# Adding the taps of a depthwise convolution by accumulating transfers, in three tiles instead of two

## The chip, the core and the metric

The kernel runs on one core of a Trainium2 chip. It uses five queues of instructions: TensorE (PE in the profile, with its weight loads as PEld), VectorE (DVE), ScalarE (ACT), GpSimd (POOL) and SyncE (SP), which issues the transfers. The metric is the device time of one execution in microseconds (us), lower is better.

## The reference

One layer of a hybrid decoder, for 1024 positions of 1024 channels in fp32: a modulated RMS norm, one wide input product, a convolution group and a recurrent group beside each other, and an output product.

```
h = rmsnorm(x, norm_g) * (1 + scale) + shift
cv, cg, cs, lx, ls = split(h @ w_in)              # five times 1024 channels

v = cv * sigmoid(cg)
v = causal_depthwise_conv(v, dw_w, dw_b)          # 31 taps a channel
v = silu(layernorm(v, cln_g, cln_b))              # over the channels
y_conv = (v @ pw2_w + pw2_b) * silu(cs)

xs = causal_depthwise_conv(lx, sc_w, sc_b)        # 4 taps
r, i = sigmoid(xs @ wr + br), sigmoid(xs @ wi + bi)   # 8 blocks of 128 channels
a = exp(-8 * r * softplus(-lam))
hs = scan(a, sqrt(1 - a * a) * i * xs)            # h_t = a_t h_{t-1} + b_t
y_lru = hs * silu(ls)

x = x + (1 + gate) * (concat(y_conv, y_lru) @ w_out)
return rmsnorm(x, final_g)
```

The change concerns the convolution of 31 taps and, in a small way, where sums stand in PSUM.

## The kernel before

Channels lie on the 128 partitions and positions along the free dimension, so every activation is eight tiles of 128 x 1024 floats. Each fp32 product is made of three products of halves: a weight tile is split by ScalarE into a rounded upper part `whi` (a cast), and by GpSimd into the rest, `wlo` = raw - `whi`; the activation has `uh` and `ul` likewise. A weight tile is then 48 matmuls of 512 columns (8 blocks of channels, three products, two halves of the positions). Raw tiles, upper and lower parts have two buffers each.

The program isn't written in the order in which it runs. Each step is recorded as an `Op` with an engine, an assumed cost, a priority and the buffers that it reads and writes, and `Plan.order` lists the steps engine by engine: whenever an engine is free it takes the ready step with the lowest priority number for which there are buffers. The order of each queue is fixed by these assumed costs; at run time each engine goes through its queue in that order and waits where an operand isn't there. A pool of 47 buffers of one tile each (`big`) holds nearly all activations, and a buffer that the plan has freed is given to the next step that needs one.

The stages, in order: loading and modulation; the first products (`first`, by blocks of `FIRST`), with the sums of squares and their spread beside them; a long stretch over `slots` of the input product, in which each slot is one weight tile; the products of the recurrent group's gates (`gate`), scans and convolutions between them; the recurrent half of the output product (slots `lru`), beside which the layer norm runs; the second product of the convolution group (`pw2`, TensorE rows `papw` and `pbpw`); and the rest of the output product with the final norm.

The convolution of one tile is recorded by `conv_tile(i)`, as soon as its input `v` is there. There are two kinds:

- Tiles in `POOLED` (2 and 5): ScalarE multiplies the shifted input with each tap (tiles `cq`), and GpSimd adds the products one after another into the tile `c`.
- The other six: VectorE sums the taps by even and odd positions with a scheme of three half-length convolutions, in an accumulator `cacc` in PSUM of two banks, 15 + 15 + 14 taps of 512 positions, with copies by ScalarE and three additions behind it.

The finished tiles are added into `csum` in the order `SUMS`, by GpSimd and the last by VectorE. TensorE multiplies `csum` with a matrix of 1/1024 (`mean`); `layer_norm` subtracts it from the eight tiles, sums the squares, spreads the reciprocal root over the partitions (`lnbc`), and `quarters` splits the results for `pw2`.

GpSimd also does `wlo`, the products of the gate's modulation (`modw`, followed by a ScalarE step that sums them up) and most of `csum`. ScalarE also does `whi`, the evacuation of product tiles (`sig`, `scs`, `sls`, `xs`), and the gates' functions with loads of function tables. PSUM has a pool of three product tiles of two banks (`mm`) and one accumulator of two banks (`acc`), which the fourth of the first products, the token statistics, the convolution sums, `mean` and `lnbc` use in turn.

In the profile, L320 is the helper `TT` (additions, subtractions and products of two tensors, on either engine), L312 the helper `STT` (VectorE, a scalar times a tensor and an addition), L301 and L293 are ScalarE's `ACT`, and L438 is the matmul of a weight tile.

Of the kernel before, what the change touches and what calls it, by code (L numbers as in the profile page):

```python
# [9 lines left out]
F32 = mybir.dt.float32  # L10
# [35 lines left out]
POOLED = (2, 5)  # L46
# [6 lines left out]
SUMS = (0, 1, 3, 2, 4, 6, 5, 7)  # L53
QRES = 4
GM = 22
# [22 lines left out]
class Op:  # L78
    __slots__ = ("eng", "cost", "emit", "prio", "table", "bufs", "succ", "wait", "ready",
                 "seq", "reserve", "columns", "lock", "end", "psum")  # L80


class Plan:
# [23 lines left out]
    def op(self, eng, cost, emit, prio, r=(), w=(), table=None, after=(), reserve=0,  # L107
           columns=0, lock=False):
        o = Op()
        o.eng, o.cost, o.emit, o.prio, o.table = eng, cost, emit, prio, table  # L110
# [24 lines left out]
        o.psum = [(b, any(k[0] is b for k in w)) for b in o.bufs if b.pool in ("mm", "acc")]  # L135
        self.ops.append(o)
        return o

    def order(self):
# [19 lines left out]
        def done(o, end):  # L159
            o.end = until[o.eng] = end  # L160
# [14 lines left out]
        while left:  # L175
# [3 lines left out]
            for e in engines:  # L179
# [42 lines left out]
                if e == "POOL" and held["DVE"] > t + 1e-9:  # L222
                    waiting, until[e] = o, float("inf")
                    continue
# [24 lines left out]
def hymba_layer(ctx: ExitStack, tc: tile.TileContext, xT, c_row, vecs, mod_w, w_first, w_in,  # L249
# [11 lines left out]
    psacc = ctx.enter_context(tc.tile_pool(name="psacc", bufs=1, space=bass.MemoryType.PSUM))  # L261
# [8 lines left out]
    pools["acc"] = (psacc, "acc", [P, T], 1)  # L270
# [46 lines left out]
    def TT(prio, eng, out, a, b, op, n=T, r=(), w=(), reserve=0, after=()):  # L317
# [3 lines left out]
                    reserve=reserve, lock=not in_psum(r), after=after)  # L321

# [132 lines left out]
    def acc_tile(name, parts=2):  # L455
        return S.buf("acc", name, F32, parts)
# [187 lines left out]
    psf = [mm_tile(f"first{n}", 4) for n in range(3)] + [acc_tile("first3", 4)]  # L644
    psb = psf[3]
# [15 lines left out]
    def fw_mm(prio, ps, i, xh, xl, k, cols, after=()):  # L661
        _, wh, wl = fw[k - k % 2]

        def emit():
            for lhs, rhs, last in ((wh, xh, 0), (wh, xl, 0), (wl, xh, 1)):
                for a, b in cols:
                    pe.matmul(ps()[:, a:b], fw_part(lhs, k, i * P, i * P + P)(),  # L667
# [92 lines left out]
    st, wk = ctile("st", KT), halves(psb, H, T)  # L760

    def stats(sq, k):
        for b in range(KT):
            pe.matmul(psb()[:, H + b:H + b + 1], sq()[:, b * P:b * P + P], ones[:, 0:1],
                      start=k == 0 and b == 0, stop=k == len(sqs) - 1, skip_group_check=True)

    def spread_mm(a, e):
        for b in range(a // P, e // P):
            o = H + b * P - a
# [4 lines left out]
    ACT(RSP, lambda: st, lambda: psb()[:, H:H + KT], AF.Sqrt, KT, bias=eps_t, scale=1.0 / D,  # L774
        r=wk, w=[("st", 0)])
    S.op("DVE", 0.12, lambda: dve.reciprocal(st, st), RSP, [("st", 0)], [("st", 0)])
    for a, e in START:
        spread = S.op("PE", 0.22 * ((e - a) // P), lambda a=a, e=e: spread_mm(a, e), RSP,
                      [("st", 0)], wk, columns=4 * (e - a))
        ACT(RSP, part(rbc, a, e), part(psb, H, H + e - a), "copy", e - a, r=wk,  # L780
# [104 lines left out]

    def conv_tile(i):
# [19 lines left out]
        acc, b2 = acc_tile(f"cacc{i}"), bias2[:, i:i + 1]  # L906
        acc_e, acc_s, src_s = half(acc, 0), half(acc, 1), half(ci, 0)
# [8 lines left out]
        def every(o):  # L916
# [3 lines left out]
            w=[(acc, 0)])  # L920
        ACT(pr, acc_s, src_s, AF.Identity, H, scale=ws(0), bias=b2,
            r=[(ci, 0), ("V", 1), ("wsum", 0)], w=[(acc, 1)])
        for r in range(1, 16):
            STT(pr, cut(acc_e, r, H), cut(ev, 0, H - r), w(2 * r), cut(acc_e, r, H), ALU.mult,
                ALU.add, H - r, r=[vi, (acc, 0)], w=[(acc, 0)])
            STT(pr, cut(acc_s, r, H), cut(src_s, 0, H - r), ws(r), cut(acc_s, r, H), ALU.mult,
                ALU.add, H - r, r=[(ci, 0), (acc, 1)], w=[(acc, 1)])
        ACT(pr, every(1), acc_s, "copy", H, r=[(acc, 1)], w=[ci])
        ACT(pr, acc_s, od, AF.Copy, H, scale=w(1), r=[vi], w=[(acc, 1)])
        for r in range(1, 15):  # L930
            STT(pr, cut(acc_s, r, H), cut(od, 0, H - r), w(2 * r + 1), cut(acc_s, r, H), ALU.mult,
                ALU.add, H - r, r=[vi, (acc, 1)], w=[(acc, 1)])
        ACT(pr, every(0), acc_e, "copy", H, r=[(acc, 0)], w=[ci])
        TT(pr, "DVE", every(1), every(1), acc_e, ALU.subtract, H, r=[ci, (acc, 0)], w=[ci])
        TT(pr, "DVE", every(1), every(1), acc_s, ALU.subtract, H, r=[ci, (acc, 1)], w=[ci])
        TT(pr, "DVE", cut(every(0), 1, H), cut(every(0), 1, H), cut(acc_s, 0, H - 1), ALU.add,
           H - 1, r=[ci, (acc, 1)], w=[ci])
# [99 lines left out]
    def layer_norm():  # L1037
        pr = 45
        mean = acc_tile("mean")
# [14 lines left out]
        bc = acc_tile("lnbc")  # L1054
# [7 lines left out]
    for i, (s, ps) in enumerate(zip(FIRST, psf)):  # L1062
        j, p, bi = s[1] % KT, EVP + i, bias[:, i:i + 1]
        t = big_buf(f"first_u{i}", parts=4)
        for a, e in START:
# [4 lines left out]
            else:  # L1070
                for k in range(KT):
                    fw_mm(RSP + 60 + 0.1 * k, ps, i, uhs[k], uls[k], k, ((a, e),), after=[spread])
                TT(p, "DVE", part(t, a, e), part(ps, a, e), part(rbc, a, e), ALU.mult, n,
                   r=pk + halves(rbc, a, e), w=tk)
# [230 lines left out]
```

## Time and profile before

| | before |
|---|---|
| runs, us | 768.59, 771.37, 770.60 (median 770.60) |
| the profiled execution, us | 771.28 |
| its span, us | 769.4 |
| mean granted TensorE clock | 0.985 |
| busy: TensorE, VectorE, ScalarE, GpSimd | 95%, 87%, 55%, 42% |
| DMA: bytes, share of the 16 engines | 77.28 MB, 28.5% |

The span runs from the first to the last instruction on the core; the execution's own time is 1.9 us more. The rows of the profile give for each group the line, the engine, the operation, the tiles as out<-in, and the shapes, then the count and the times. A tile name without its number stands for all buffers of that name. Weight loads (PEld) run beside the matmuls.

### The profile page before, as it was taken

Reading aid. Unit: us, or ns where it says so; the run is one execution under the profiler, and the core shown is the slowest. Engines: PE = TensorE matmul, PEld = TensorE weight load, DVE = VectorE, ACT = ScalarE, POOL = GpSimd, SP = SyncE. Lnnn points to the kernel's source line nnn. Section 1 sums busy time; section 2 is a strip of 40 time slices with the busy share of each in tenths; the row PEclk is TensorE's granted clock in tenths of the full one; section 3 lists DMA queues with packets and bytes.
Section 4 is the critical chain, followed back from the end, with each engine's and each line's share of the span. In section 5 each row is a group of like instructions: output and inputs, shape, how many; then the busy total and the mean of one; then the engine's idle time right before and its main releaser. Section 6 shows DMA issues by size and latency. Waiting matters only on the chain.

```text
span 769.4 us, 8629 instructions
## 1 busy us (share of the span) xinstructions
PE 733.5 (95%) x3288; PEld 606.0 (79%) x3288; DVE 665.6 (87%) x806; ACT 420.3 (55%) x473; POOL 323.1 (42%) x132
## 2 busy tenths in 40 slices
PE   3999899999999997999999998999999999999995
PEld 2888677888888885888888787788888888887885
DVE  7999999789899889999897998995977666999565
ACT  6630926997626477955956565664723223455220
POOL 0030312799899469989999612121220000000000
PEclk9999999999999999899999999999999999999997
DMA  9930221102102312331111012433332621425114
GB/s 329 406 118 32 83 82 35 55 27 83 63 28 83 116 55 83 116 110 56 55 55 55 27 55 81 138 136 111 136 115 96 200 110 40 152 83 177 43 55 164
DMA packets 24954, 77.84 MB, mean 101 GB/s; under 512 B 2768, under 2 KB 6096, under 8 KB 24912
## 3 DMA queue, kind: packets, MB, share of 16 engines
q1 hardware_dynamic: 24912, 77.28, 28.5%
q8 instruction: 26, 0.43, 0.2%
q14 instruction: 16, 0.13, 0.1%
HBM read 64.68 MB, written 12.58 MB: 100 GB/s over the span
## 4 chain that ended last, share of the span: by engine, by line
PE 57%; DVE 29%; ACT 7%; POOL 3%; issue 2%; DMA 1%; SPq 0%; DVEq 0%; ACTq 0%; POOLq 0%
PE ps L438 32%; DVE cacc L312 11%; PE first L667 6%; PE papw L559 5%; PE pbpw L559 4%; PE out L605 3%; ACT cq L301 3%; PE paout L559 2%; DVE r L1020 2%; PE pbout L559 2%; DVE xs L312 1%; DVE xs L320 1%; DVE yl L320 1%; DVE sls L320 1%; POOL c L320 1%
## 5 line engine op out<-in xcount | busy, mean ns | idle before, releaser
L320 POOL TENSOR_TENSOR wlo<-raw,whi 128x1024 fp32r<-128x1024 f32 x44 | 115.1, 2615 | 234.5 <-ACT whi L293 234.5
L438 PE MATMUL ps<-uh,whi 128*128 128x512 f32 x576 | 180.5, 395 | 7.0 <-ACT scs L301 6.6
L438 PE MATMUL ps<-ul,whi 128*128 128x512 f32 x576 | 179.7, 393 | 3.6 <-DVE ul L312 3.6
L438 PE MATMUL ps<-uh,wlo 128*128 128x512 f32 x576 | 179.3, 393 | 1.6 <-POOL wlo L320 1.6
L320 POOL TENSOR_TENSOR c<-c,cq 128x1023 f32<-128x1023 f32 (+29 forms) x60 | 159.8, 2663 | 9.5 <-ACT cq L301 7.0
L312 DVE SCALAR_TENSOR_TENSOR cacc<-v,V,cacc 128x511 f32<-128x511 f32 (+14 forms) x174 | 129.6, 745 | 13.7 <-ACT c L293 6.3
L438 PEld LDWEIGHTS ps<-uh,whi 128*128 128x128 f32 x576 | 109.4, 191 | 31.4 <-ACT scs L301 7.5
L438 PEld LDWEIGHTS ps<-ul,whi 128*128 128x128 f32 x576 | 109.3, 190 | 27.7 <-DVE ul L312 4.7
L438 PEld LDWEIGHTS ps<-uh,wlo 128*128 128x128 f32 x576 | 109.2, 190 | 24.8 <-POOL wlo L320 2.0
L293 ACT CAST whi<-raw 128x1024 fp32r<-128x1024 f32 x48 | 50.3, 1047 | 59.6 <-issue 34.4
L301 ACT ACTIVATE cq<-sig,V 128x1023 f32<-128x1023 f32 (+29 forms) x60 | 63.9, 1128 | 1.6 <-POOL c L320 1.6
L312 DVE SCALAR_TENSOR_TENSOR cacc<-c,wsum,cacc 128x511 f32<-128x511 f32 (+6 forms) x84 | 62.7, 746 | 2.3
L301 ACT ACT_TABLE_LOAD x45 | 57.7, 1283 | 1.6 <-PEq L1297 0.7
L438 PE MATMUL ps<-yh,whi 128*128 128x512 f32 x128 | 39.6, 391 | 0.0
L438 PE MATMUL ps<-yh,wlo 128*128 128x512 f32 x128 | 39.4, 389 | 0.0
L438 PE MATMUL ps<-yl,whi 128*128 128x512 f32 x128 | 39.4, 389 | 0.0
L667 PE MATMUL first<-uh,fhi 128*128 128x512 f32 x64 | 26.7, 416 | 11.1 <-ACT uh L301 11.1
L312 DVE SCALAR_TENSOR_TENSOR xs<-ps,V,xs 128x1023 f32<-128x1023 f32 (+2 forms) x24 | 30.6, 1274 | 2.6 <-ACT xs L301 2.5
L438 PEld LDWEIGHTS ps<-yl,whi 128*128 128x128 f32 x128 | 24.0, 188 | 5.0
L438 PEld LDWEIGHTS ps<-yh,wlo 128*128 128x128 f32 x128 | 24.0, 188 | 5.0
L667 PE MATMUL first<-ul,fhi 128*128 128x512 f32 x64 | 26.3, 411 | 1.7 <-DVE ul L312 1.7
L438 PEld LDWEIGHTS ps<-yh,whi 128*128 128x128 f32 x128 | 23.9, 188 | 4.9
(299 smaller groups left out, 1359.7 us busy)
## 6 DMA issues: line engine op xcount, KB each, us to landing
raw<-in_w_in_dram SPq DMA_DIRECT2D x36, 512.0 KB, 3.3
modw<-in_mod_w_dram SPq DMA_DIRECT2D x24, 512.0 KB, 7.8
raw<-in_w_out_dram SPq DMA_DIRECT2D x12, 512.0 KB, 3.9
scsd<-scs SPq DMA_DIRECT2D x8, 512.0 KB, 2.6
acc<-in_xT_dram SPq DMA_DIRECT2D x8, 512.0 KB, 4.6
accd<-acc SPq DMA_DIRECT2D x8, 512.0 KB, 2.8
rawpw<-in_pw_dram SPq DMA_DIRECT2D x8, 512.0 KB, 3.8
scsr<-scsd SPq DMA_DIRECT2D x8, 512.0 KB, 5.3
```

The lines of the kernel that those rows point to most:

```text
L293: act.copy(out(), in_())
L301: act.activation(out=out(), in_=in_(), func=func, **kw)
L312: dve.scalar_tensor_tensor(out=out(), in0=in0(), scalar=scalar, in1=in1(), op0=op0, op1=op1, accum_out=accum)
L320: lambda: e.tensor_tensor(out=out(), in0=a(), in1=b(), op=op), prio, r, w,
L438: pe.matmul(ps()[:, a - off:b - off], k3(lhs)()[:, k, :], rhs[k]()[:, a:b], start=(k == 0 and lhs is wh and rhs is xh and (a - off) % H == 0),
L559: pe.matmul(half(*ps)(), half(*lhs)()[:, j * P:j * P + P], half(*rhs)(), start=start and j == 0 and z == 0, stop=j == KT // 2 - 1 and z == ...
L605: pe.matmul(ps()[:, a - off:e - off], k3(lhs)()[:, k, :], rhs()[:, i * H + a % H:i * H + a % H + e - a], start=k == KORD[0] and lhs is wh ...
L667: pe.matmul(ps()[:, a:b], fw_part(lhs, k, i * P, i * P + P)(), rhs()[:, a:b], start=k == 0 and lhs is wh and rhs is xh, stop=k == KT - 1 a ...
L1020: S.op("DVE", 2.2, lambda: dve.tensor_tensor_scan(out=r(), data0=a(), data1=xs(), initial=0.0, op0=ALU.mult, op1=ALU.add), pr, [a, xs], [r])
```

## The change

Tile 4 joins `POOLED`, so five tiles are left for VectorE. In the pooled tiles the products aren't added by GpSimd's arithmetic: GpSimd issues a transfer from the product `cq` into the sum that adds while it writes (`accum_op`). There are two sums a tile: `c` takes the even taps and `d` the odd ones, tap 1 is written straight into `d`, and a last accumulating transfer adds `d` to `c`. Each transfer into a sum waits for the one before it in the same sum. The plan assumes 1.2 us of GpSimd's time for an issue and 6.0 us more until it has landed (`lag`), and a product of ScalarE is not begun before the third-last addition is planned to have landed (`AHEAD`). An issue isn't kept apart from VectorE's work by the plan's `lock`, as GpSimd's arithmetic is.

The PSUM accumulators are of one bank each, two of them. The sums over even positions and over the pairs get one each; the fourth of the first products has one for its first half, and a new one, `late`, for its second; the token statistics have their own; `mean` and `lnbc` move to the product tiles. In the tiles of VectorE the copy of the even sums and the first subtraction come ahead of the odd taps. `SUMS` has another order.

```
-POOLED = (2, 5)
+POOLED = (2, 4, 5)
-SUMS = (0, 1, 3, 2, 4, 6, 5, 7)
+SUMS = (0, 1, 3, 2, 6, 4, 7, 5)
+AHEAD = 3
+ISSUE, LAND = 1.2, 6.0
...
-        o.lock = eng == "POOL" or eng == "DVE" and lock
+        o.lock = not lag and eng == "POOL" or eng == "DVE" and lock
...
-            o.end = until[o.eng] = end
+            until[o.eng] = end
+            o.end = end = end + o.lag
...
-    pools["acc"] = (psacc, "acc", [P, T], 1)
+    pools["acc"] = (psacc, "acc", [P, H], 2)
...
+    def ADD(prio, out, a, n=T, r=(), w=(), after=()):
+        return S.op("POOL", ISSUE, lambda: pool.dma_start(out(), a(), accum_op=ALU.add), prio, r,
+                    w, lag=LAND * n / T, after=after)
...
         if i in POOLED:
             ACT(pr, ci, vi, AF.Identity, scale=w(0), bias=vec("dw_b", i), r=[vi, ("V", 1)],
                 w=[ci])
+            adds, sums = [], [ci, big_buf(f"d{i}")]
             for s in range(1, TAPS):
-                q = big_buf(f"cq{i}_{s}")
+                q = sums[1] if s == 1 else big_buf(f"cq{i}_{s}")
                 ACT(pr, part(q, s, T), part(vi, 0, T - s), AF.Copy, T - s, scale=w(s), r=[vi],
-                    w=[q], reserve=QRES)
-                TT(pr, "POOL", part(ci, s, T), part(ci, s, T), part(q, s, T), ALU.add, T - s,
-                   r=[ci, q], w=[ci])
+                    w=[q], reserve=QRES, after=adds[-AHEAD:][:len(adds) // AHEAD][:1])
+                if s > 1:
+                    to = sums[s % 2]
+                    adds.append(ADD(pr, part(to, s, T), part(q, s, T), r=[to, q], w=[to]))
+            ADD(pr, part(ci, 1, T), part(sums[1], 1, T), r=sums, w=[ci])
             c[i] = ci
             return
-        acc, b2 = acc_tile(f"cacc{i}"), bias2[:, i:i + 1]
-        acc_e, acc_s, src_s = half(acc, 0), half(acc, 1), half(ci, 0)
+        acc, acs, b2 = acc_tile(f"cacc{i}"), acc_tile(f"caccs{i}"), bias2[:, i:i + 1]
+        acc_e, acc_s, src_s = half(acc, 0), half(acs, 0), half(ci, 0)
...
-        mean = acc_tile("mean")
+        mean = mm_tile("mean")
...
-        bc = acc_tile("lnbc")
+        bc = mm_tile("lnbc")
...
+                late = acc_tile("late")
                 for k in range(KT):
-                    fw_mm(RSP + 60 + 0.1 * k, ps, i, uhs[k], uls[k], k, ((a, e),), after=[spread])
+                    fw_mm(RSP + 60 + 0.1 * k, late, i, uhs[k], uls[k], k, ((a, e),),
+                          after=[spread], off=a)
```

More of the change, by code (lines that the diff above doesn't have):

```diff
@@ L221, in order @@
                         free[b.pool] -= 1
-                if e == "POOL" and held["DVE"] > t + 1e-9:
+                if e == "POOL" and o.lock and held["DVE"] > t + 1e-9:
                     waiting, until[e] = o, float("inf")
@@ L453, in mm_tile, with acc_tile @@
         return S.buf("mm", name, F32, parts)
[L455 to L456 removed]
+    def acc_tile(name):
+        return S.buf("acc", name, F32)
     def half(b, i):
@@ L643, in hymba_layer @@
     sc = big_buf("sc")
-    psf = [mm_tile(f"first{n}", 4) for n in range(3)] + [acc_tile("first3", 4)]
-    psb = psf[3]
+    psf = [mm_tile(f"first{n}", 4) for n in range(3)] + [acc_tile("first3")]
+    psb = acc_tile("token_stats")
     cuts = [START, START, START, START[:1]]
@@ L779, in hymba_layer @@
                       [("st", 0)], wk, columns=4 * (e - a))
-        ACT(RSP, part(rbc, a, e), part(psb, H, H + e - a), "copy", e - a, r=wk,
+        ACT(RSP, part(rbc, a, e), part(psb, 0, e - a), "copy", e - a, r=wk,
             w=halves(rbc, a, e))
@@ L1070, in hymba_layer @@
             else:
+                late = acc_tile("late")
                 for k in range(KT):
-                    fw_mm(RSP + 60 + 0.1 * k, ps, i, uhs[k], uls[k], k, ((a, e),), after=[spread])
-                TT(p, "DVE", part(t, a, e), part(ps, a, e), part(rbc, a, e), ALU.mult, n,
-                   r=pk + halves(rbc, a, e), w=tk)
+                    fw_mm(RSP + 60 + 0.1 * k, late, i, uhs[k], uls[k], k, ((a, e),),
+                          after=[spread], off=a)
+                TT(p, "DVE", part(t, a, e), part(late, 0, n), part(rbc, a, e), ALU.mult, n,
+                   r=[late] + halves(rbc, a, e), w=tk)
             if s[1] < CG:
```

45 lines of the change are left out of this document (24 added, 21 removed).

## The prediction

> **What bounds the kernel now.** I read the page first, then the windows of single stretches, then who waited for whom, then the chain of waits ahead of the longest stall, and last the rows of the tiles that the change touches. The page:
>
> ```profile
> span 769.4 us, 8629 instructions
> PE 733.5 (95%) x3288; PEld 606.0 (79%) x3288; DVE 665.6 (87%) x806; ACT 420.3 (55%) x473; POOL 323.1 (42%) x132
> PE 57%; DVE 29%; ACT 7%; POOL 3%; issue 2%; DMA 1%; SPq 0%; DVEq 0%; ACTq 0%; POOLq 0%
> ```
>
> TensorE is busy 733.5 of 769.4 us, so only its stalls can be won. What a stall costs is read from its pace. In the chain (start, length, what) an undisturbed weight tile is this row:
>
> ```profile
> 65.36 10.89 PE ps L438 x48
> ```
>
> 48 matmuls in 10.89 us: 0.2269 us each, 10.9 us for a weight tile. The windows give for each stretch the busy time and, in brackets, the matmuls that began in it; width minus count times 0.2269 is what was lost, idle time and slow clock together:
>
> ```profile
> 88.00:102.00 14.00, 10.42 (x37) 7.62 (x36) 14.00 (x18) 9.42 (x13) 2.76 (x1) 0.88 0.32 112
> 286.00:292.00 6.00, 4.42 (x20) 3.33 (x19) 5.93 (x7) 6.00 (x8) 6.00 (x4) 1.00 0.08 10
> 303.00:313.00 10.00, 5.81 (x16) 4.28 (x15) 9.54 (x14) 9.37 (x11) 9.84 (x6) 0.66 0.33 120
> 474.00:481.00 7.00, 4.59 (x14) 3.33 (x13) 4.85 (x7) 6.90 (x8) 2.38 (x1) 0.76 0.44 149
> 120.00:285.00 165.00, 165.00 (x730) 136.60 (x729) 149.27 (x159) 110.18 (x115) 126.77 (x51) 1.00 0.19 64
> ```
>
> From 120 to 285 us 730 x 0.2269 = 165.6 of 165 us: nothing is lost. Lost are 14 - 8.4 = 5.6 us at 88:102, 6 - 4.5 = 1.5 at 286:292, 10 - 3.6 = 6.4 at 303:313 (a clock of 0.66 follows the stall) and 7 - 3.2 = 3.8 at 474:481. The last three, 11.7 us, lie in the stage of the convolution sums. Who was waited for (total, times, longest):
>
> ```profile
> PE ps L438 <- ACT scs L301: 6.6, 2, 4.2
> ACT modw L301 <- POOL modw L320: 15.5, 5, 7.2
> ACT c L293 <- DVE cacc L312: 17.1, 3, 7.0
> ```
>
> Both long stalls end with ScalarE clearing a product tile (scs) late, because its queue stood behind a wait for GpSimd (modw, 303) or for VectorE's taps (c from cacc, 474). The chain into the stall at 303 shows it:
>
> ```profile
> 295.45 3.34 POOL c L320
> 298.78 2.36 POOL wlo L320
> 301.14 2.37 POOL modw L320
> 303.53 1.16 ACT modw L301 x2
> ...
> 306.98 0.93 ACT scs L301
> 307.95 2.08 PE ps L438 x4
> ```
>
> GpSimd's queue is full (9.84 of 10 us at 303:313); each step in it is a 2.4 us addition. So the bound is TensorE, and the loss within reach comes from GpSimd and VectorE running late in this stage.
>
> **The change part by part.** Rows of the steps that it touches (duration min/median/max in ns, first and last start):
>
> ```profile
> L320 POOL TENSOR_TENSOR c<-c,cq x60: 2329/2382/4346, 138.3 to 421.3; 128x1023 f32<-128x1023 f32 x2, 128x1022 f32<-128x1022 f32 x2, 128x1021 f32<-128x1021 f32 x2, 128x1020 f32<-128x1020 f32 x2
> L312 DVE SCALAR_TENSOR_TENSOR cacc<-c,wsum,cacc x84: 708/746/753, 108.4 to 471.6; 128x511 f32<-128x511 f32 x6, 128x510 f32<-128x510 f32 x6, 128x509 f32<-128x509 f32 x6, 128x508 f32<-128x508 f32 x6
> L293 ACT COPY c<-cacc x12: 602/618/637, 144.2 to 475.3; 128x512 f32<-128x512 f32 x12
> L320 DVE TENSOR_TENSOR c<-c,cacc x18: 656/687/696, 150.2 to 495.1; 128x512 f32<-128x512 f32 x12, 128x511 f32<-128x511 f32 x6
> ```
> ```profile
> L301 ACT ACTIVATE cq<-sig,V x60: 1111/1128/1147, 137.1 to 393.7; 128x1023 f32<-128x1023 f32 x2, 128x1022 f32<-128x1022 f32 x2, 128x1021 f32<-128x1021 f32 x2, 128x1020 f32<-128x1020 f32 x2
> ```
> ```profile
> L1020 DVE TENSOR_TENSOR_SCAN r<-a,xs x8: 2271/3830/4382, 135.8 to 491.2; 128x1024 f32<-128x1024 f32 x8
> ```
> ```profile
> 130.00:490.00 360.00, 351.55 (x1530) 289.21 (x1529) 330.77 (x335) 242.87 (x255) 282.08 (x109) 0.99 0.20 67
> 230.00:375.00 145.00, 139.23 (x604) 114.36 (x603) 135.18 (x150) 99.90 (x114) 123.75 (x50) 0.98 0.25 87
> 0.00:20.00 20.00, 7.22 (x17) 5.34 (x18) 14.55 (x46) 13.33 (x18) 0.70 (x6) 1.00 0.91 331
> ```
>
> *VectorE.* Tile 4 leaves it: 15 + 15 + 14 taps by the code, 44 x 0.746 = 32.8, three additions of 0.687 = 2.1, one of the halves about 0.7: -35.6 us. VectorE falls from 330.8 of the 360 us from 130 to 490 (92%) to 295 (82%). The scan takes 2.27 us at best and 3.83 in the median, which I read as VectorE waiting beside GpSimd's additions; 8 x 1.56 = 12.5 us of that may go too. None of it is on the path by itself; it is what makes ACT's wait for the taps at 474 unlikely to return.
>
> *GpSimd.* 60 additions go, 60 x 2.38 = 143 us. 90 issues come (per tile taps 2 to 30 and one joining of the two sums; tap 1 is written straight into the second sum). No GpSimd issue is in this trace. Its price is bounded below by an SP issue and above by the addition it replaces (2.38):
>
> ```profile
> L334 SPq DMA_DIRECT2D modw<-in_mod_w_dram x24: 327/328/527, 2.1 to 337.2; - x24
> ```
>
> 0.33 to 2.38 us; I take 1.2, near the middle and what the new plan itself assumes. 108 us come: GpSimd falls from 282 to 247 of 360 us (bounds 169 and 353).
>
> *ScalarE.* 31 products more, 31 x 1.128 = 35.0, minus the tile's two copies and three starts at 0.618 at least, 3.1: +31.9 us, from 243 to 275 of 360 us (76%). It is covered as long as the products, which have the lowest priority, go into its gaps; at 76% that holds on average, not everywhere.
>
> *The transfers.* Each sum is a chain: an addition waits until the one before it in the same sum has landed. Landing of 512 KB (issues, median us):
>
> ```profile
> raw<-in_w_in_dram SPq DMA_DIRECT2D x36, 512.0 KB, 3.3
> scsd<-scs SPq DMA_DIRECT2D x8, 512.0 KB, 2.6
> ...
> x<-in_xT_dram SPq DMA_DIRECT2D x7, 512.0 KB, 10.0
> ```
>
> Bounds are 2.6 us (a plain store) and 10.0 us (the loads of the first 20 us, when the engines were 91% busy). An addition also has to read its target: 3.3 + one more reading (0.524 MB at 331 GB/s = 1.6) + as much again for the sister sum in flight = 6.5 us. With the issue a step is 7.7 us, and 15 steps a sum make 116 us for a tile. In the built order of the changed kernel the third tile's sums begin about where tile 5's begin now and end just ahead of `mean`; tile 5's GpSimd additions now end at 421 us. There is room for 15 steps of even 14 us. The chains by themselves cost nothing.
>
> What waits behind them does: GpSimd's queue is in order, so an addition that waits for a landing holds the `wlo` subtraction that TensorE needs next, and in the built program 83 ScalarE instructions wait for a landing too, because they reuse buffers that the plan frees at its assumed 6.0 us. At 6.5 us I cost this at one short stall, 3 us; at 10 us it is the second rival.
>
> *The place of mean.* In the built order `mean` stands 54 rows of two matmuls later than now, 54 x 2 x 0.2269 = 24.5 us, and as much less work is left between it and the second convolution products. Now:
>
> ```profile
> 499.18 1.98 PE mean L1043 x4
> ```
> ```profile
> 570.22 0.69 DVE L320 TENSOR_TENSOR vla<-vu,vha 128x512 fp32r<-128x512 f32 x1 [0.69 <-ACT vha L293]
> ```
> ```profile
> 593.28 5.44 PE papw L559 x24
> ```
>
> The last lower part that the second of these products needs (vla) is ready at 570.9 and wanted at 593.3 + 2.7 = 596.0: 25 us of cover, of which 24.5 go. Without the three stalls TensorE gets to `mean` at 499.2 - 11.7 + 24.5 = 512. Until then the sums must be done; from there on the layer norm has next to no cover, and each us that it is late is a us of the total. I cost it at nothing, with up to 5 us in the range.
>
> *PSUM.* Accumulators of one bank, `mean` and `lnbc` in the product pool, `late` and `token_stats` apart: no instruction more, and the order of TensorE's rows at the start is the same. While `mean` is read TensorE has two product tiles instead of three, each 10.9 us of work, in which the tile before has to be cleared: nothing, unless VectorE lets it wait that long.
>
> The sum: 771.3 (the profiled execution; 769.4 is its span) - 11.7 + 3.0 = 762.6. The median of the runs is 770.6, 0.7 lower: **762 us**.
>
> **The rivals.** *The stalls move.* ScalarE at 76%, or the layer norm without cover, gives back what is won: 10 us of 11.7, 769 to 770. For it: the two long stalls already end on ScalarE. Against: ScalarE was late there because it waited, not because it was full.
>
> *The transfers fill the DMA engines; this one ends slower.* In the built order 52 of the 90 additions lie between 13 successive `wlo` tiles. TensorE's work there is 13 x 10.89 + 3 gate pairs of 12 x 0.2269 = 150 us. The DMA price is from this row (packets, MB, share of 16 engines' span):
>
> ```profile
> q1 hardware_dynamic: 24912, 77.28, 28.5%
> ```
>
> 28.5% of 769.4 us for 77.28 MB: 1.49 us of all engines for 0.524 MB. The stage carries 25% (230:375) already, 38 us. With one pass an addition, 52 x 1.49 + 38 = 115 of 150 us, and it fits. With two passes, 52 x 2.98 + 38 = 193: 43 us too much. GpSimd's two `wlo` buffers let it be one tile (10.9) ahead, and 11.7 us of lateness replace today's stalls: 43 - 10.9 - 11.7 = +20 us, 771.3 + 20 - 0.7 = 791. It decides from (150 - 38) / 52 = 2.2 us an addition. For it: an addition must read source and target. Against: whether reading and writing share the 1.49 us is not in the trace. The Trainium skill ("Collectives: The Full Stack", The bandwidth ceiling) has the rule that speaks for this rival: an adding transfer is slower than a copy not for the addition but because its two source reads go through the same ring, 31 against 62 GB/s. By that rule the 791 would be the forecast; no row of this trace shows an adding transfer.
>
> *The issue costs as much as the addition did.* In the same 13 tiles 52 x 2.38 + 13 x 2.36 + 8 x 2.37 (modw) + 2 x 2.4 (csum) = 178 of 150 us on GpSimd; minus the same 10.9 and 11.7: +5 us, 776.
>
> **How the numbers follow.** Forecast 0.54: the losses have named causes in GpSimd's and VectorE's queues, and both get lighter. Moved stalls 0.10; full DMA engines 0.28, a little over half of the forecast's, since one pass and two are both open; costly issue 0.08. What a measurement of this kernel can tell from no change is 0.5%, 3.9 us. So faster 0.54, same 0.10, slower 0.28 + 0.08 = 0.36. The low end is all three stalls and the 5.6 us at 88:102 gone and nothing new, 771.3 - 17.3 - 0.7 = 753; the high end takes in the second rival with 3 us of lost cover, 794. The forecast's own range is 753 to 767.
>
> **What would show it.** Right: the issues on GpSimd near 1.2 us, landings of the additions near 6.5, the three windows without loss, VectorE about 36 us and more lighter, `mean` on TensorE near 512 us with no wait ahead of it. Wrong: GpSimd's `wlo` behind additions that wait for landings, a DMA share near 9 tenths from about 230 to 375 us, ScalarE waiting for DMA ahead of its tile evacuations, or TensorE idle ahead of `mean` or of the first `papw`.

## The result, and the profile after

| | before | after |
|---|---|---|
| runs, us: median (lowest to highest) | 770.3 (768.6 to 771.4) | 790.1 (788.1 to 795.4) |
| ratio, 95% interval | | 1.027 (1.022 to 1.032) |
| the profiled execution and its span, us | 771.3, 769.4 | 790.0, 788.2 |
| mean granted TensorE clock (1 is full speed) | 0.985 | 0.977 |
| busy: TensorE, VectorE, ScalarE, GpSimd, us | 733.5, 665.6, 420.3, 323.1 | 738.8, 604.5, 450.2, 236.8 |
| DMA: GpSimd's queue; all the others | none; 77.28 MB, 28.5% | 46.48 MB, 31.4%; 77.28 MB, 28.2% |

The kernel is slower by 20 us, at the time of the second rival (791). In its profile the helpers stand a few lines further on: L324 is `TT`, L316 `STT`, L305 and L297 `ACT`, L447 the matmul of a weight tile, and L329 the issue of an addition. Lines of the page after: the span, the busy times, the DMA share in 40 slices of 19.7 us (tenths), and the queues (packets, MB, share of 16 engines' span):

```profile
span 788.2 us, 8776 instructions
PE 738.8 (94%) x3288; PEld 608.1 (77%) x3288; DVE 604.5 (77%) x758; ACT 450.2 (57%) x499; POOL 236.8 (30%) x162
DMA  8930312797899999999968414494324440424114
q0 software_dynamic: 12960, 46.48, 31.4%
q1 hardware_dynamic: 24912, 77.28, 28.2%
```

VectorE and GpSimd have less to do than before, and the DMA engines are what is new: from slice 12 to slice 20 (217 to 394 us) the row stands at 9 throughout. 90 additions took 31.4% of 788.2 us: 247.5 us, or **2.75 us of all engines an addition**. The windows of the stage (busy us and, in brackets, matmuls begun; after the engines the granted clock, the DMA share, GB/s):

```profile
130.00:490.00 360.00, 340.46 (x1467) 278.59 (x1466) 267.65 (x282) 255.25 (x266) 188.11 (x133) 0.97 0.83 183
230.00:375.00 145.00, 128.56 (x543) 104.38 (x542) 72.41 (x69) 103.31 (x115) 89.90 (x66) 0.94 1.02 228
```

From 130 to 490 us 360 - 1467 x 0.2269 = 27.1 us of TensorE are lost, where before it was 12.8. In 230:375 alone it is 145 - 543 x 0.2269 = 21.8 (before 8.0), at a DMA share of 1.02 (full; the profile's sum can come out a little above 1) and with VectorE half idle. Who waited for whom (total us, times, longest):

```profile
ACT modw L305 <- POOL modw L324: 28.0, 7, 9.0
POOL c L329 <- DMA c<-cq: 19.9, 8, 6.4
DVE csum L324 <- DMA c<-d: 11.8, 1, 11.8
POOL d L329 <- DMA d<-cq: 9.0, 5, 4.1
```

and of these TensorE's own:

```profile
PE ps L447 <- ACT scs L305: 10.5, 1, 10.5
PE ps L447 <- POOL wlo L324: 5.9, 4, 2.3
PE mean L1058 <- DVE csum L324: 3.0, 1, 3.0
```

GpSimd waits for landings (19.9 and 9.0 us), ScalarE for GpSimd's modw (28.0, before 15.5), TensorE for ScalarE's scs (10.5) and for wlo (5.9). How they hang together is seen in the timeline of the longest stall (start, length, engine; in brackets the idle time before it and what ended it):

```profile
303.80 0.86 POOL L329 DMA_DIRECT2D c<-cq  x1 [4.83 <-DMA d<-cq]
306.57 0.86 POOL L329 DMA_DIRECT2D d<-cq  x1 [1.92 <-PE gate L1023]
...
310.04 2.96 POOL L324 TENSOR_TENSOR modw<-modw,sc 128x1024 f32<-128x1024 f32 x1
...
313.04 1.06 ACT L305 ACTIVATE modw<-modw 128x1024 f32<-128x1024 f32 x1 [5.61 <-POOL modw L324]
...
315.12 1.00 ACT L305 ACTIVATE scs<-ps 128x1024 f32<-128x1024 f32 x1
...
316.18 1.22 PE L447 MATMUL ps<-uh,whi 128*128 128x512 f32 x2 [10.52 <-ACT scs L305]
```

By the timeline the first issue held GpSimd's queue for 4.83 us, until a transfer into the sister sum (`d` of the same tile) had landed; why the program makes an addition into `c` wait for one into `d` is not shown. The gate's modulation (modw) stood behind it, ScalarE waited 5.61 us for that, and only then cleared the product tile that TensorE had been waiting for since 305.7. It is the stall that the kernel before had at the same place, longer, with a landing at its root where there was an addition. A slower clock follows it (granted 0.69 in the mean from 303 to 325 us), so that 13.4 us of work are lost there, counted from the starts of the matmuls, as all losses of a single stall below.

At the end of the stage the chain ahead of `mean`:

```profile
528.06 9.71 DMA c<-d
...
537.95 1.96 DVE csum L324
...
540.04 3.48 PE mean L1058 x4
```

The transfer that joins the last tile's two sums lands at 537.8, VectorE adds it, and TensorE has waited 3.0 us; its four matmuls then take 3.48 us instead of 0.9. With before's 1.98 for the same four that is 4.5 us more. The stage lost 27.1 - 12.8 = 14.3 us more than before, and 14.3 + 4.5 = 18.8 us is the whole difference of the spans.

### The profile page after: what moved, and what is told of

Same layout as the page of the kernel before. It is cut to its first block, busy times and chain, and to the rows that moved or that the text cites. A ratio compares the mean times of both kernels' runs of the same rounds, so it can differ in the third digit from the quotient of the medians.

```text
span 788.2 us, 8776 instructions
## 1 busy us (share of the span) xinstructions
PE 738.8 (94%) x3288; PEld 608.1 (77%) x3288; DVE 604.5 (77%) x758; ACT 450.2 (57%) x499; POOL 236.8 (30%) x162
## 3 DMA queue, kind: packets, MB, share of 16 engines
q0 software_dynamic: 12960, 46.48, 31.4%
q1 hardware_dynamic: 24912, 77.28, 28.2%
## 4 chain that ended last, share of the span: by engine, by line
PE 60%; DVE 18%; DMA 7%; issue 6%; ACT 5%; POOL 4%; SPq 0%; DVEq 0%; POOLq 0%; ACTq 0%
PE ps L447 34%; PE first L676 5%; PE papw L568 5%; PE pbpw L568 4%; DMA modw<-in_mod_w_dram 4%; DVE caccs L316 3%; PE paout L568 3%; PE out L614 2%; DMA c<-d 2%; PE pbout L568 2%; DVE xs L316 2%; PE gate L1023 1%; DVE xs L324 1%; ACT cq L305 1%; POOL modw L324 1%
## 5 line engine op out<-in xcount | busy, mean ns | idle before, releaser
L447 PE MATMUL ps<-uh,whi 128*128 128x512 f32 x576 | 180.1, 394 | 10.9 <-ACT scs L305 10.5
L447 PE MATMUL ps<-uh,wlo 128*128 128x512 f32 x576 | 180.0, 394 | 5.9 <-POOL wlo L324 5.9
L447 PE MATMUL ps<-ul,whi 128*128 128x512 f32 x576 | 180.0, 394 | 3.6 <-DVE ul L316 3.6
L324 POOL TENSOR_TENSOR wlo<-raw,whi 128x1024 fp32r<-128x1024 f32 x44 | 118.8, 2700 | 204.8 <-ACT whi L297 201.6
L447 PEld LDWEIGHTS ps<-uh,whi 128*128 128x128 f32 x576 | 109.6, 191 | 34.7 <-ACT scs L305 10.9
L447 PEld LDWEIGHTS ps<-uh,wlo 128*128 128x128 f32 x576 | 109.2, 190 | 30.3 <-POOL wlo L324 7.6
L447 PEld LDWEIGHTS ps<-ul,whi 128*128 128x128 f32 x576 | 109.4, 190 | 27.7 <-DVE ul L316 4.7
L305 ACT ACTIVATE cq<-sig,V 128x1010 f32<-128x1010 f32 (+25 forms) x87 | 94.3, 1127 | 3.0 <-DMA d<-cq 2.9
L297 ACT CAST whi<-raw 128x1024 fp32r<-128x1024 f32 x48 | 50.1, 1044 | 49.1 <-issue 26.1
L329 POOL DMA_DIRECT2D c<-cq x45 | 42.9, 981 | 59.5 <-ACT cq L305 16.4
L329 POOL DMA_DIRECT2D d<-cq x42 | 40.7, 984 | 53.8 <-PE ps L447 11.7
L316 DVE SCALAR_TENSOR_TENSOR cacc<-v,V,cacc 128x511 f32<-128x511 f32 (+14 forms) x75 | 55.4, 739 | 0.3 <-ACT cacc L305 0.3
L316 DVE SCALAR_TENSOR_TENSOR caccs<-v,V,caccs 128x511 f32<-128x511 f32 (+6 forms) x70 | 52.2, 745 | 1.3
L316 DVE SCALAR_TENSOR_TENSOR caccs<-c,wsum,caccs 128x511 f32<-128x511 f32 (+6 forms) x70 | 51.8, 740 | 0.6
L316 DVE SCALAR_TENSOR_TENSOR xs<-ps,V,xs 128x1023 f32<-128x1023 f32 (+2 forms) x24 | 30.6, 1273 | 23.2 <-ACT xs L305 23.1
L324 DVE TENSOR_TENSOR xs<-g,xs 128x1024 f32<-128x1024 f32 x8 | 12.4, 1544 | 40.1 <-ACT g L305 40.1
L447 PE MATMUL ps<-yh,whi 128*128 128x512 f32 x128 | 40.6, 399 | 0.0
L447 PE MATMUL ps<-yl,whi 128*128 128x512 f32 x128 | 39.4, 389 | 0.0
L447 PE MATMUL ps<-yh,wlo 128*128 128x512 f32 x128 | 39.4, 389 | 0.0
L316 DVE SCALAR_TENSOR_TENSOR r<-a,r 128x1024 f32<-128x1024 f32 x8 | 14.2, 1773 | 26.9 <-ACT r L305 26.9
L676 PE MATMUL first<-uh,fhi 128*128 128x512 f32 x56 | 23.4, 417 | 11.0 <-ACT uh L305 11.0
```

The costliest lines, as they stand in the source:

```text
L297: act.copy(out(), in_())
L305: act.activation(out=out(), in_=in_(), func=func, **kw)
L316: dve.scalar_tensor_tensor(out=out(), in0=in0(), scalar=scalar, in1=in1(), op0=op0, op1=op1, accum_out=accum)
L324: lambda: e.tensor_tensor(out=out(), in0=a(), in1=b(), op=op), prio, r, w,
L329: return S.op("POOL", ISSUE, lambda: pool.dma_start(out(), a(), accum_op=ALU.add), prio, r, w, lag=LAND * n / T, after=after)
L447: pe.matmul(ps()[:, a - off:b - off], k3(lhs)()[:, k, :], rhs[k]()[:, a:b], start=(k == 0 and lhs is wh and rhs is xh and (a - off) % H == 0),
```

## The experiments

Theory A: the additions fill the DMA engines, at two passes of the data each; everything else follows from it. Its rivals: that the landings cost it (latency in an in-order queue), whatever the engines carry; and that the new order of the steps costs it (the mean 24.5 us later, ScalarE's 31 products more, the PSUM part). The quoted expectations give each theory a letter and say what it is. All ratios are to the kernel before on the same chip.

**Half the bytes.** In the issue of an addition, with the order and the count of the instructions kept; the right half of the columns is not summed:

```
-pool.dma_start(out(), a(), accum_op=ALU.add)
+pool.dma_start(out()[:, :n // 2], a()[:, :n // 2], accum_op=ALU.add)
```

> Every accumulating transfer moves only the first half of its columns (the other half of each product is left out of the sum); issues, waits and the order of all queues are those of the changed kernel. Theory A, the additions fill the DMA engines (2.75 us of all engines each, 31.4% of 788.2 us for 90): the price halves, the share of 230 to 375 us falls from 1.02 to about 0.65, landings fall from 7.3 us to below 5, and the time to 760 to 768 us. Theory B, one addition simply takes longer to land (7.3 us) than the plan's 6.0, whatever its size: landings stay at 6.5 us or more and the time above 783 us. Theory C, the cost is that of the other parts (PSUM accumulators, ScalarE's 31 products, the later mean): 783 to 790 us with landings below 5 us.

760.2 us (758.4 to 761.8), ratio 0.984 (0.980 to 0.989). The window and GpSimd's queue:

```profile
230.00:375.00 145.00, 145.00 (x642) 120.05 (x640) 89.65 (x91) 126.24 (x137) 103.66 (x73) 1.00 0.75 171
```
```profile
q0 software_dynamic: 12960, 23.60, 17.8%
```

642 x 0.2269 = 145.7: TensorE loses nothing in 230:375. Order, issues, waits and ScalarE's products are those of the changed kernel, so the rival of the order falls: all of the loss hangs on what the transfers carry. Whether by full engines or by later landings this run can't tell, since the landings became shorter too (4.4 us in the median, 7.3 in the changed kernel). The DMA share, 0.75, is above the 0.65 that was expected.

**Plain copies.** The same transfers without adding, so that the sums hold their last product only:

```
-pool.dma_start(out(), a(), accum_op=ALU.add)
+pool.dma_start(out(), a())
```

> The transfers copy and don't add (so the sums hold only the last product); bytes, issues, waits and order are those of the changed kernel. Theory A in the form of two passes (an addition reads its source and its target): a copy takes half of the engines' time, 1.4 us, the share of 230 to 375 us falls to about 0.65 and the time to 760 to 770 us. If the engines are filled by the bytes or by the packets alone, and adding is free: share about 1.0 and 785 to 795 us, as with the additions. Theory B: landings stay at 6.5 us or more, above 783 us. Theory C: 783 to 790 us with short landings.

760.2 us (757.0 to 764.5), ratio 0.983 (0.978 to 0.988).

```profile
q0 software_dynamic: 7200, 46.48, 15.1%
```
```profile
230.00:375.00 145.00, 145.00 (x641) 120.05 (x641) 88.95 (x92) 124.06 (x137) 83.46 (x71) 1.00 0.73 266
```

15.1% of 762.7 us for 90 transfers: 1.28 us of all engines a copy, 7200 / 90 = 80 packets where an addition has 12960 / 90 = 144. The bytes written are the same; adding raises 1.28 to 2.75. The packets alone aren't the price: with half the columns they are as many, 12960, at 1.50 us an addition.

**The transfers by themselves.** A kernel of 64 transfers of 512 KB that GpSimd issues, without the layer: 8 additions into one sum (tile `onesum`, L31), 24 into four sums in turn (`foursums`, L35), 8 copies into one tile (`onecopy`, L39), 24 into four (`fourcopies`, L43):

```
+for _ in range(6):
+    for t in tb:
+        pool.dma_start(t, sb, accum_op=ALU.add)
```

> Only transfers of 512 KB issued by GpSimd, the layer is left out: 8 additions into one sum, 24 into four sums in turn, 8 plain copies into one tile, 24 copies into four tiles. Theory A (an addition takes two passes of the engines): with four in flight 2.6 to 2.9 us an addition and 1.2 to 1.5 us a copy; in one chain 4.5 to 5.5 us a step for additions and 3 to 4 for copies. If the price in the changed kernel came from the collision with its other transfers, additions alone would take 1.3 to 2.0 us at four in flight.

Starts of issues in its timeline, two of each part where it runs evenly (in brackets the idle time before; `issue` means that nothing in the profile ends it):

```profile
38.52 0.86 POOL L31 DMA_DIRECT2D onesum<-srca  x1 [4.03 <-DMA onesum<-srca]
43.38 0.85 POOL L31 DMA_DIRECT2D onesum<-srca  x1 [4.00 <-DMA onesum<-srca]
...
88.83 0.89 POOL L35 DMA_DIRECT2D foursums<-srcb  x1 [1.85 <-issue]
91.52 0.87 POOL L35 DMA_DIRECT2D foursums<-srcb  x1 [1.80 <-issue]
...
137.15 0.53 POOL L39 DMA_DIRECT2D onecopy<-srcc  x1 [2.66 <-DMA onecopy<-srcc]
140.38 0.53 POOL L39 DMA_DIRECT2D onecopy<-srcc  x1 [2.71 <-DMA onecopy<-srcc]
...
176.40 0.53 POOL L43 DMA_DIRECT2D fourcopies<-srcd  x1 [0.76 <-DMA fourcopies<-srcd]
177.69 0.53 POOL L43 DMA_DIRECT2D fourcopies<-srcd  x1 [0.76 <-DMA fourcopies<-srcd]
```

and the windows inside the two parts with four tiles (DMA share and GB/s at the end):

```profile
60.00:110.00 50.00, 0.00 (x0) 15.72 (x19) 1.00 1.06 199
164.00:180.00 16.00, 0.00 (x0) 6.37 (x12) 1.00 1.01 391
```

Four sums take 2.69 us an addition, one sum 4.86; copies 1.29 and 3.23. In both windows the engines are full, at 199 GB/s of additions and 391 of copies. So the price is the addition's own and not the collision with weights. The rule in the Trainium skill ("Collectives: The Full Stack", The bandwidth ceiling), that an adding transfer is limited by its two source reads through one ring, at half the copy's rate, agrees: 199 to 391 here, there 31 to 62 GB/s. What no run here shows is that it is the ring; twice the engines' time is what they show.

The additions were not four in flight, as the expectation has it: by their landing times never more than three are under way, where the copies reach four. From the fourth on, each issue stood 1.7 to 2.3 us, though its own sum was free, and began 0.31 us after a landing. In the changed kernel six issues stood in the same way, 13.5 us in all, one of them just behind the stall above:

```profile
318.74 0.88 POOL L329 DMA_DIRECT2D d<-cq  x1 [3.86 <-issue]
```

So GpSimd's queue was also held ahead of a fourth addition, whatever sum it went to; with two tiles (a run below), where at most two are under way, no issue stood like this. How much of the loss goes by this wait and how much by the waits for a landing in the same tile (28.9 us) was not separated.

**Between half and all.** Three quarters and seven eighths of the columns, the rest not summed (one line for each kernel, in place of the issue of an addition):

```
+pool.dma_start(out()[:, :n * 3 // 4], a()[:, :n * 3 // 4], accum_op=ALU.add)
...
+pool.dma_start(out()[:, :n * 7 // 8], a()[:, :n * 7 // 8], accum_op=ALU.add)
```

> Every addition moves three quarters of its columns (the last quarter of the sums is left out); order, issues and ScalarE's products are those of the changed kernel. Theory A (the DMA engines' time is what the additions cost, it hurts from about 2.2 us of all engines an addition): between 1.50 us at half the bytes and 2.75 at all of them, three quarters take about 2.1 us an addition; 52 x 2.1 + 38 = 147 of 150 us between 230 and 375 us, which just fits: DMA share 0.88 to 0.95 there and a time of 760 to 766 us. Theory B (a cost in proportion to the bytes, without a threshold): halfway between 760 and 790, 772 to 778 us.

> Every addition moves seven eighths of its columns (the last eighth of the sums is left out). Theory A: about 2.4 us an addition, above the 2.2; 52 x 2.4 + 38 = 163, 13 us more than the 150 of TensorE: 764 (with one tile of 10.9 us of weights ahead) to 775 us, DMA share 0.97 to 1.02 in 230:375. Theory B (in proportion to the bytes): 780 to 784 us.

```profile
q0 software_dynamic: 12960, 35.40, 24.9%
```
```profile
230.00:375.00 145.00, 143.79 (x634) 118.65 (x633) 91.38 (x91) 123.53 (x135) 99.37 (x73) 1.00 0.97 219
```
```profile
q0 software_dynamic: 12960, 41.29, 28.4%
```
```profile
230.00:375.00 145.00, 135.40 (x587) 110.65 (x587) 75.49 (x79) 112.97 (x126) 93.87 (x70) 0.98 1.01 225
```

| columns moved | us of all engines an addition | DMA share, 230:375 | TensorE lost, 230:375 | time, us (lowest to highest) |
|---|---|---|---|---|
| half | 17.8% x 757.0 / 90 = 1.50 | 0.75 | 0 | 760.2 (758.4 to 761.8) |
| three quarters | 24.9% x 765.1 / 90 = 2.12 | 0.97 | 1.1 | 767.2 (765.5 to 769.0) |
| seven eighths | 28.4% x 775.1 / 90 = 2.45 | 1.01 | 11.8 | 777.4 (776.5 to 778.5) |
| all | 31.4% x 788.2 / 90 = 2.75 | 1.02 | 21.8 | 790.1 (788.1 to 795.4) |

The knee in 230:375 stands where the engines become full, between 2.12 and 2.45. Both times came between the bands of the two theories: 767.2 is 1.2 above A's and 777.4 is 2.4 above it, and both are below the bands of a cost in proportion. A cost in proportion to the bytes it isn't: the step from half to three quarters costs 7.0 us, the one from three quarters to all 22.9. But it isn't free below the knee either: at three quarters `mean` waits 2.99 us, and its four matmuls take 2.91 instead of 0.9:

```profile
516.25 2.91 PE L1058 MATMUL mean<-csum,ones_d 128*128 128x512 f32 x4 [2.99 <-DVE csum L324]
```

VectorE's addition ahead of it (csum) waited for the last joining transfer there too.

**Two tiles by transfers.** `POOLED` and `SUMS` as before, all else as changed:

```
-POOLED = (2, 4, 5)
+POOLED = (2, 5)
-SUMS = (0, 1, 3, 2, 6, 4, 7, 5)
+SUMS = (0, 1, 3, 2, 4, 6, 5, 7)
```

> The changed kernel with tiles 2 and 5 only by accumulating transfers, tile 4 on VectorE as before, and the old order of the sum over tiles. Theory A: 60 additions of 2.75 us, and the tiles hardly overlap; the share of 230 to 375 us stays below 0.8 and the time falls to 762 to 772 us. Theory B: each chain still lands late, 775 to 785 us. Theory C with ScalarE as its cause: 765 to 772 us, with PSUM as its cause: above 783 us.

761.7 us (760.7 to 762.9), ratio 0.986 (0.982 to 0.990).

```profile
POOL d L329 <- DMA d<-cq: 17.3, 5, 5.6
POOL c L329 <- DMA c<-cq: 14.7, 5, 5.4
```
```profile
230.00:375.00 145.00, 144.66 (x639) 119.44 (x638) 118.90 (x137) 112.39 (x126) 89.00 (x57) 1.00 0.83 191
```

GpSimd's issues wait 32.0 us for landings, more than in the changed kernel (28.9), and 145 - 639 x 0.2269 = 0 is lost. So waiting for landings by itself is not the cost. The time is just under the expected range, the share just above it (0.83 for 0.8).

**The PSUM part without transfers.** The kernel after with before's two tiles and GpSimd's additions in them: accumulators of one bank, `mean` and `lnbc` in the product tiles, `late` and the token statistics apart, the moved steps in VectorE's tiles:

```
-POOLED = (2, 4, 5)
+POOLED = (2, 5)
...
-                if s > 1:
-                    to = sums[s % 2]
-                    adds.append(ADD(pr, part(to, s, T), part(q, s, T), r=[to, q], w=[to]))
-            ADD(pr, part(ci, 1, T), part(sums[1], 1, T), r=sums, w=[ci])
...
+                TT(pr, "POOL", part(ci, s, T), part(ci, s, T), part(q, s, T), ALU.add, T - s,
+                   r=[ci, q], w=[ci])
```

> The changed kernel with two tiles whose products GpSimd adds with its own arithmetic, as before; what is left of the change is PSUM accumulators of one bank, mean and lnbc in the product tiles, late and token_stats, and the moved steps in VectorE's tiles. Theories A and B: no cost in these, 764 to 774 us (before 770.3). Theory C with PSUM as its cause: above 780 us.

**759.9 us** (759.3 to 761.6), ratio 0.984 (0.980 to 0.988): faster than both kernels, below the 764 to 774 that was expected, and the fastest median of all kernels here that leave nothing out.

```profile
230.00:375.00 145.00, 145.00 (x642) 120.05 (x641) 130.15 (x148) 108.48 (x123) 128.76 (x51) 1.00 0.24 86
```
```profile
ACT modw L305 <- POOL modw L324: 14.7, 4, 5.6
```

The stalls at 286 and 303 are gone although GpSimd has as much to do as before (128.76 us in 230:375, before 123.75). ScalarE's wait for VectorE's taps (before 17.1 us, `c` from `cacc`) is no longer in the list at all, with VectorE busy 130.15 us there, before 135.18. I read it so that with one accumulator the next tile's sums had to wait until ScalarE had emptied it; what is shown is that the wait goes with this part, and with the order of the queues that the plan makes of it. The part costed at nothing is worth 10.5 us, and two tiles by transfers (761.7) bring nothing beyond it.

**Which part of it.** Three kernels: the last one with the copy of the even sums (ScalarE) and the first subtraction (VectorE) back in their old places; before with those two steps moved and nothing else; before with `mean` and `lnbc` in the product tiles and nothing else:

```
-        ACT(pr, every(0), acc_e, "copy", H, r=[acc], w=[ci])
-        TT(pr, "DVE", every(1), every(1), acc_e, ALU.subtract, H, r=[ci, acc], w=[ci])
...
+        ACT(pr, every(0), acc_e, "copy", H, r=[acc], w=[ci])
+        TT(pr, "DVE", every(1), every(1), acc_e, ALU.subtract, H, r=[ci, acc], w=[ci])
```

> As e4_psum_only (759.9 us), but with VectorE's steps in their old order: the copy of the even sums and the first subtraction behind the odd taps. If the moved steps are what makes e4 10.5 us faster than before (ScalarE's wait for the taps ahead of the stall at 474 us): 768 to 772 us. If the accumulators of one bank are: 758 to 763 us.

> The kernel before with only the moved steps: the copy of the even sums and the first subtraction ahead of the odd taps. If these make the gain of e4: 759 to 764 us. If the accumulators of one bank do: 768 to 773 us. In between if each makes a part.

> The kernel before with one edit: mean and lnbc stand in the product tiles instead of the accumulator. If the gain of the PSUM part (759.9 us) comes from the accumulators of one bank: 769 to 772 us, as before. If it comes from mean and lnbc leaving the accumulator: below 766 us.

Old places: 765.6 us (761.4 to 770.1 in ten runs), ratio 0.993 (0.990 to 0.996). Moved steps alone: 770.2, ratio 0.999 (0.997 to 1.002). `mean` and `lnbc` alone: 769.9, ratio 0.999 (0.997 to 1.001). The kernel with the old places lies between its two expected ranges. Neither of the small edits does anything alone; the accumulators of one bank, with `late` and the statistics apart and `mean` and `lnbc`, which are two banks wide, in the product tiles, bring about 5 us and, with the moved steps, which give the first bank back sooner, about 10.5. `late` was not tried apart from the accumulators, as it is there because of them.

**Half of the additions by transfer.** Three tiles, the odd taps by transfer and the even ones, and the joining, by GpSimd's arithmetic:

```
-                    adds.append(ADD(pr, part(to, s, T), part(q, s, T), r=[to, q], w=[to]))
-            ADD(pr, part(ci, 1, T), part(sums[1], 1, T), r=sums, w=[ci])
+                    if s % 2:
+                        adds.append(ADD(pr, part(to, s, T), part(q, s, T), r=[to, q], w=[to]))
+                    else:
+                        TT(pr, "POOL", part(to, s, T), part(to, s, T), part(q, s, T), ALU.add,
+                           T - s, r=[to, q], w=[to])
+            TT(pr, "POOL", part(ci, 1, T), part(ci, 1, T), part(sums[1], 1, T), ALU.add, T - 1,
+               r=sums, w=[ci])
```

> Three tiles as in the changed kernel, but only the odd taps are added by transfers (42 instead of 87); the even taps and the joining of the two sums are GpSimd additions. Theory A (two passes fill the DMA engines): 42 x 2.75 = 115 us of engines instead of 247, the share of 230 to 375 us near 0.65, and 758 to 766 us. If the third tile on ScalarE is a cost too: 768 us or more. If GpSimd is filled instead (48 x 2.4 + 42 x 0.9 = 153 us beside its other work): 768 to 778 us with TensorE waiting for wlo.

783.3 us (782.5 to 784.1), ratio 1.015 (1.011 to 1.020): a miss. The engines are not full, and it is slow all the same:

```profile
230.00:375.00 145.00, 136.52 (x593) 111.76 (x592) 111.66 (x88) 107.28 (x122) 117.60 (x62) 0.98 0.63 157
```
```profile
255.33 13.38 DVE L316 SCALAR_TENSOR_TENSOR r<-a,r 128x1024 f32<-128x1024 f32 x1 [4.14 <-ACT r L305]
...
291.89 15.82 DVE L324 TENSOR_TENSOR xsl<-xs,xsh 128x1024 fp32r<-128x1024 f32 x1 [1.23 <-ACT xsh L297]
```
```profile
PE gate L1028 <- DVE xsl L324: 6.1, 1, 6.1
PE papw L568 <- DVE wlopw L324: 5.8, 1, 5.8
PE papw L568 <- DVE l34pw L324: 3.4, 1, 3.4
```

Two losses of another kind. VectorE's lower part for a gate (xsl) takes 15.82 us, at a time in which GpSimd has additions and wlo directly behind one another, and TensorE waits 6.1 us for it (7.9 with the slow clock). And `mean` comes so close to the second convolution products (99 rows of TensorE ahead of `papw`, 141 in the changed kernel) that the layer norm has no cover: 9.2 us of waiting, 14.0 with the clock. So A's price does not say that fewer transfers are fast; it says only what they cost the engines.

**Joining by arithmetic.** Only the last transfer of a tile, `d` into `c`, goes back to GpSimd's arithmetic:

```
-            ADD(pr, part(ci, 1, T), part(sums[1], 1, T), r=sums, w=[ci])
+            TT(pr, "POOL", part(ci, 1, T), part(ci, 1, T), part(sums[1], 1, T), ALU.add, T - 1,
+               r=sums, w=[ci])
```

> The changed kernel with the joining of the two sums of a tile done by GpSimd's arithmetic, the 87 additions left as transfers. In the changed kernel csum waited 11.8 us for the last joining transfer and TensorE lost 5.9 us at mean. If that wait is a cost of its own: 4 to 6 us less than the changed kernel, 784 to 786 us. If lateness only moves to the place where the additions before it land: within 2 us of 790.

790.7 us (789.8 to 791.4), ratio 1.024 (1.019 to 1.030). The wait ahead of `mean` is gone and its microseconds are lost earlier (8.3 around 430 us, where the changed kernel loses 4.6): while the engines are behind, the place at which it shows is not a cost of its own.

## Why the prediction was wrong

The steps in their order.

*What bounds the kernel.* Right: TensorE's stalls in this stage could be won, and when they go the kernel stands at 760, 10.5 us lower, against the 11.7 that the windows gave.

*Which edit would take them away.* Wrong in its attribution. The prediction had them go because GpSimd and VectorE lose work to ScalarE and to transfers. They go without that, by the PSUM part alone (759.9), which was "costed at nothing". The row for it had been read: ScalarE's 17.1 us of waiting for the taps in `cacc` were put down to VectorE's load, and they went with VectorE's load little changed (647.0 us over the span, before 665.6).

*VectorE.* -35.6 us and perhaps 12.5 more was forecast; it is 61.1 lighter (665.6 to 604.5). Right in sign, and of no use, since VectorE did not set the end.

*GpSimd's issues.* Priced at 1.2 us between 0.33 and 2.38; the rows say 0.88 in the median, and about a quarter of them take longer, up to 1.55:

```profile
L329 POOL DMA_DIRECT2D c<-cq x45: 847/877/1534, 134.7 to 519.0; - x45
L329 POOL DMA_DIRECT2D d<-cq x42: 852/877/1548, 135.7 to 517.1; - x42
DMA to landing us min/median/max: 4.5/7.3/11.7
```

The third rival (the issue as costly as the addition) is out. *ScalarE:* +29.9 us for +31.9. *Landing:* 6.5 forecast, 7.3 in the median and 11.7 at worst; alone on the engines a step of one chain is 4.86 with its issue, and with half the columns the landing is 4.4 in the median, so the rest comes with the load.

*The transfers.* This is the step that failed. The forecast gave them 3 us, "one short stall", from the landing time alone; the runs show about 30, from 760.2 us with half of the columns moved to 790.1 with all. It put their work on the engines into a rival, with one pass or two left open and the chance given to one. An addition takes 2.75 us of all engines, close to the 2.98 of two passes and above the deciding 2.2, and the knee was found between 2.12 and 2.45. To weigh two passes lower than one was a choice without a row behind it: that an addition reads its target was already in the landing estimate of the step before, where the second reading was counted at full price. The same reading had to be counted on the engines. The rule of the Trainium skill ("Collectives: The Full Stack", The bandwidth ceiling) stood beside the rival and said as much; the runs agree with it, 2.75 to 1.28 us.

*The rival's own sum.* It hit 791 by luck, by two errors that cancel. Its price was too high, 2.98 for 2.75: 52 x 2.75 + 38 = 181, 31 us too much and not 43, which with its deductions, 22.6 us, would have been 779. And one deduction, 10.9 us for the tile of wlo ahead, does not show: the longest wait came in through modw and scs, not through wlo's buffers. The other, 11.7 us for the lateness that was there already, did come, but from the PSUM part, which took the stalls away (10.5 us). From that level of 760, with nothing more deducted, the same formula gives 760 + 31 = 791 for all columns (790.1), 760 + 15 = 775 for seven eighths (777.4), and 760 for three quarters (767.2), where it misses the wait of `mean`. That the 10.9 are lost rather than something else is read from these sums, not tested.

*The place of mean.* It was to come at 512 us and came at 540, because of the losses ahead of it (27.1 us from 130 to 490, and its own wait of 3.0): with half the bytes it came at 511.4. The cover of 25 us was said to fall to nothing: TensorE reached the first `papw` at 611.3 with no wait ahead of it, so 141 rows are still enough, and 99 are not (783.3).

*What would show it.* The signs named for the rival are in the trace: wlo and modw behind additions that wait for landings, a DMA share above 9 tenths from 230 to 375 us, TensorE idle ahead of `mean`. ScalarE waited ahead of its tile evacuations too, but for GpSimd's modw (5.61 us in the longest stall) much more than for a landing (1.64 us there); ahead of the first `papw` TensorE did not wait.

## What to carry to other kernels

Before arithmetic is moved into transfers, put the transfers into the busiest stretch of the profile, not into the span, and count an addition as two copies of its bytes (2.7 against 1.3 us of all engines for 512 KB): here the share over the whole span was 60%, and the engines were full for 145 us of it. When an edit bundles a resource that is split (here one accumulator of two banks into two of one) with work that is moved, price the split by the wait that ends on that resource, and run it alone: it was the whole gain. A change that gives VectorE and GpSimd less to do can be slower, since in-order queues carry the lateness of a landing to the engine that matters.

## What was not expected of the hardware

An instruction of VectorE that reads two SBUF tiles, 1.2 us long by itself, can stand for the length of several GpSimd instructions in a row: 13.38 us (r, at 255.3) beside five of them, of which the last ended at 267.6, and 15.82 us (xsl, at 291.9) beside six, both in the run with half of the additions by transfer. In the kernel before the longest of these two kinds took 1.81 and 3.36. The Trainium skill ("SBUF — State Buffer", SBUF: two separate sides) has the lock between the two engines, held for the whole instruction of the one that starts first. The trace agrees as to the lock, and shows more: most of GpSimd's instructions there start 2.35 us apart and each is recorded as 2.9, so that no gap is left in which VectorE gets its turn; that this is the reason is a reading, not tested.

An accumulating transfer has 144 packets where a copy of the same bytes has 80, and its issue takes GpSimd 0.88 us instead of 0.54 (medians). Three such additions are the most that are under way at once in any run here; the next issue stands, and GpSimd's queue with it, until one has landed.
